# A masked-autoencoder loss on one core: squares over pairs of columns, loads and engine orders from a timetable

## The chip, the core and the metric

The kernel runs on one core of a Trainium2 chip. The metric is the time of one execution on the device, in microseconds (us), as the median of several runs. Engines are named as the profile names them: PE multiplies matrices, PEld loads its weights, DVE is VectorE, ACT is ScalarE, POOL is GpSimd, SP is SyncE. Loads from HBM run on 16 DMA engines; POOL or SP issues them.

## What is computed

Two fp32 arrays of 32 x 147 rows with 768 values each come in, `pred` and `target`. Each target row is normalised by its own mean and variance, the squared difference to the prediction row is averaged, and then the 147 rows of a batch entry are averaged:

```python
mean = target.mean(axis=-1, keepdims=True)
var = target.var(axis=-1, keepdims=True)
target = (target - mean) / np.sqrt(var + 1e-6)
loss = np.mean((pred - target) ** 2, axis=-1)
return loss.mean(axis=-1).astype(np.float32)
```

## The kernel before

**Tiling.** Four rows of each batch entry lie side by side, so 32 x 4 = 128 partitions hold one row each. This text calls one such set of 128 rows, 768 values wide, a *column*. There are 36 full columns (0 to 35) and a rest, column 36, of 32 x 3 = 96 rows. The target is loaded in pieces: the rest, then nine pieces of four columns, named t0, t4 up to t32 in the program by their first column. The prediction comes as the rest (p36), eight pieces of four columns (p0 to p28), one of two (p32) and two of one (p34, p35). The profile cuts the numbers off and writes `t` and `p`. `load` (L60) issues every piece from POOL, and the DMA turns fp32 into bf16 on the way.

**One column's way.** `stats` (L113) takes a group, as a rule four columns: for each of them DVE makes two half-row statistics (L125) and joins them (L126); ACT takes the square root of the group's variances (L127, out `r`); DVE makes the reciprocal (L129) and minus mean times reciprocal (L130, `nmr`). `normalise` (L140) then has POOL write the normalised column `s` in bf16 (L147). `losses` (L156) has PE subtract: two passes over the column, of 512 and 256 values each, one with minus the identity on `s` and one with the identity on `p`, into a PSUM tile `z` of two banks (L167; three such tiles). ACT squares `z` and sums it along the row into one value of `rl` (L169); reading the accumulator is a second record in the profile. After each prediction piece PE sums `rl` over the rows of a batch entry by a mask, into `acc` (L173). At the end DVE adds the four columns of `acc` (L190) and SP stores 32 values (L191).

**Order.** Every engine executes its instructions in order. The calls are written piece by piece: statistics and normalisation of one target piece, then subtraction, squares and the sum of the prediction piece that is due. `pin` (L57) fixes the place of the loads and normalisations on POOL; the rest is placed by the framework's scheduler. The loads stand in the order t36, t0, p36, t4, t8, p0, t12, p4 and so on; eight are issued at the start, and further ones at the first and fourth normalisation of a group (L150). There are eight semaphores for POOL's loads: each issue from the ninth on waits until the load eight before it has landed, if that is not known yet.

Of the kernel before, what the change touches and what calls it, by code (L numbers as in the profile page):

```python
# [14 lines left out]
def kernel(  # L15
# [7 lines left out]
    nc = tc.nc  # L23
    B, N, D = pred.shape
# [8 lines left out]
    BANK = 512  # L33

# [3 lines left out]
    def main_rows(x, k0, k1):  # L38
        return bass.AP(tensor=x.tensor, offset=x.offset + k0 * D,
                       ap=[[N * D, B], [KJ * D, J], [1, (k1 - k0) * D]])  # L40

    def rest_rows(x):
        return bass.AP(tensor=x.tensor, offset=x.offset + KM * D,
                       ap=[[N * D, B], [KJ * D, J - 1], [1, D]])

    data = ctx.enter_context(tc.tile_pool(name="data", bufs=1))
    work = ctx.enter_context(tc.tile_pool(name="work", bufs=20))
    small = ctx.enter_context(tc.tile_pool(name="small", bufs=6))
    singles = ctx.enter_context(tc.tile_pool(name="singles", bufs=1))
    psum = ctx.enter_context(tc.tile_pool(name="psum", bufs=3, space=bass.MemoryType.PSUM))  # L50
# [6 lines left out]
    pin = tc.keep_in_program_order  # L57
    tbuf, pbuf = {}, {}

    def load(kind, piece):  # L60
        x = targ_f if kind == "t" else pred_f
        k0, k1 = piece if piece else (KM, KM + 1)
        rows = P if piece else RP
        dt = BF16 if kind == "t" else BF16
        til = data.tile([P, (k1 - k0) * D], dt, name=f"{kind}{k0}")
        eng = nc.gpsimd if kind == "t" else nc.gpsimd
        pin(eng.dma_start(out=til[:rows], in_=main_rows(x, k0, k1) if piece else rest_rows(x)))  # L67
        for k in range(k0, k1):
            (tbuf if kind == "t" else pbuf)[k] = (til, (k - k0) * D, rows)

    eps_t = singles.tile([P, 1], F32)
    nc.vector.memset(eps_t, eps)  # L72

    load("t", t_pieces[0])
    load("t", t_pieces[1])
    load("p", p_pieces[0])
    load("t", t_pieces[2])
    load("t", t_pieces[3])
# [3 lines left out]
    for til, v in ((ident, 1.0), (nident, -1.0)):  # L82
        nc.gpsimd.memset(til, 0.0)
        nc.gpsimd.affine_select(out=til, in_=til, compare_op=ALU.not_equal, fill=v,  # L84
                                base=0, pattern=[[-1, P]], channel_multiplier=1)
    masks = {}
    for name, per, rows in (("main", J, P), ("rest", J - 1, RP)):
        m = singles.tile([P, B], F32, name=f"mask_{name}")
        nc.gpsimd.memset(m, 1.0 / (N * D))
        nc.gpsimd.affine_select(out=m[:rows], in_=m[:rows], compare_op=ALU.is_ge, fill=0.0,  # L90
                                base=0, pattern=[[-per, B]], channel_multiplier=1)
        nc.gpsimd.affine_select(out=m[:rows], in_=m[:rows], compare_op=ALU.is_ge, fill=0.0,
                                base=per - 1, pattern=[[per, B]], channel_multiplier=-1)
        masks[name] = m

    seq = []
    for i in range(4, len(t_pieces)):
        seq += [("p", p_pieces[i - 3]), ("t", t_pieces[i])]
    seq += [("p", q) for q in p_pieces[len(t_pieces) - 3:]]
    todo = iter(seq)  # L100

    def load_next():
        nxt = next(todo, None)
        if nxt is not None:
            load(*nxt)

    for _ in range(3):
        load_next()

    acc = psum1.tile([B, 4], F32)  # L110
    rs = {}

    def stats(piece):  # L113
        k0, k1 = piece if piece else (KM, KM + 1)
        rows = P if piece else RP
        K = k1 - k0
        r = small.tile([P, K], F32, name="r")
        nmr = small.tile([P, K], F32, name="nmr")
        if norm_pix_loss:
            mv = small.tile([P, K, 2], F32, name="mv")  # L120
            for k in range(k0, k1):
                til, o, _ = tbuf[k]
                st = small.tile([P, 2, 6], F32, name="st")
                for j in range(2):
                    nc.vector.bn_stats(out=st[:rows, j, :], in_=til[:rows, o + j * half:o + (j + 1) * half])  # L125
                nc.vector.bn_aggr(out=mv[:rows, k - k0], in_=st[:rows])  # L126
            nc.scalar.activation(out=r[:rows], in_=mv[:rows, :, 1], func=ACTF.Sqrt,  # L127
                                 bias=eps_t[:rows], scale=1.0)
            nc.vector.reciprocal(out=r[:rows], in_=r[:rows])  # L129
            nc.vector.scalar_tensor_tensor(out=nmr[:rows], in0=mv[:rows, :, 0], scalar=-1.0,  # L130
                                           in1=r[:rows], op0=ALU.mult, op1=ALU.mult)
        else:
            nc.vector.memset(r, 1.0)
            nc.vector.memset(nmr, 0.0)
        for k in range(k0, k1):
            rs[k] = (r[:rows, k - k0:k - k0 + 1], nmr[:rows, k - k0:k - k0 + 1])

    sbuf = {}

    def normalise(piece):  # L140
        k0, k1 = piece if piece else (KM, KM + 1)
        rows = P if piece else RP
        for k in range(k0, k1):
            r, nmr = rs[k]
            til, o, _ = tbuf[k]
            s = work.tile([P, D], BF16, name="s")
            pin(nc.gpsimd.tensor_scalar(out=s[:rows], in0=til[:rows, o:o + D], scalar1=r, scalar2=nmr,  # L147
                                        op0=ALU.mult, op1=ALU.add))
            sbuf[k] = s
            if k == k0 or k == k0 + 3:  # L150
                load_next()

    n_acc = [0]
    total_acc = len(p_pieces)

    def losses(piece):  # L156
        k0, k1 = piece if piece else (KM, KM + 1)
        rows = P if piece else RP
        K = k1 - k0
        rl = small.tile([P, 4], F32, name="rl")  # L160
        for k in range(k0, k1):
            s = sbuf[k]
            ptil, po, _ = pbuf[k]
            z = psum.tile([P, 2 * BANK], F32, name="z")
            for src, so, w, first in ((s, 0, nident, True), (ptil, po, ident, False)):
                for c0, c1 in ((0, BANK), (BANK, D)):
                    nc.tensor.matmul(z[:rows, c0:c1], w[:rows, :rows], src[:rows, so + c0:so + c1],  # L167
                                     start=first, stop=not first)
            nc.scalar.activation(out=z[:rows, :D], in_=z[:rows, :D], func=ACTF.Square,  # L169
                                 accum_out=rl[:rows, k - k0:k - k0 + 1])  # L170
        if K < 4:
            nc.vector.memset(rl[:, K:], 0.0)
# [13 lines left out]
    for pp in p_pieces[len(t_pieces) - 1:]:  # L186
        losses(pp)
# [39 lines left out]
```

## Time and profile before

| | us |
|---|---|
| median of 3 runs | 89.34 (89.18 to 89.64) |
| the profiled execution | 89.54 |
| its span, first to last instruction | 87.8 |
| busy: PE / DVE / ACT / POOL | 41.1 / 43.4 / 35.3 / 49.7 |

Numbers of the trace are microseconds from the span's start. A timeline row reads: start, length, engine, line, operation, out<-in, count, and in brackets the idle time of the engine before it with what ended it. A row of the waits reads: who waited, for whom, then total, number of times, longest. A chain row reads: start, length, what. A row of a table by stretch reads: the stretch, its length, busy time and number of records, granted PE clock, share of the DMA engines, GB/s written. A group row reads: line, engine, operation, out<-in, shapes, count, then busy us, mean ns of one, and idle time before.

### The profile page before, as it was taken

The numbers are of one execution on the slowest core, as the hardware profiler recorded it, in microseconds if no ns is written. First come the engines' busy times: TensorE is split into PE (matmuls) and PEld (weight loads), VectorE is DVE, ScalarE is ACT, GpSimd is POOL, SyncE is SP. The second block draws the span as 40 slices with busy tenths as digits, with TensorE's granted clock in tenths as the row PEclk, the third lists the DMA queues.
The fourth block names the chain that finished last, engine by engine and source line by source line (L and its number), as shares of the span: only waits on it lengthen the run. The fifth ranks groups of instructions, "written<-read, shape, count | busy, mean of one in ns | idle before, by whom it ended". The sixth has DMA issues, their size and how long they took to land.

```text
span 87.8 us, 755 instructions
## 1 busy us (share of the span) xinstructions
PE 41.1 (47%) x172; PEld 18.4 (21%) x172; DVE 43.4 (49%) x139; ACT 35.3 (40%) x86; POOL 49.7 (57%) x73
## 2 busy tenths in 40 slices
PE   0000060000495349659847255962005998999400
PEld 0000020000241124214214012420003544454200
DVE  0051989999598379339609817930991000000000
ACT  5010001010501940780492095050084678999900
POOL 4994332999999998398089469339428600000000
PEclk9999999999999955555589965579555569999995
DMA  0899999999999999999999999999999940000000
GB/s 0 120 213 201 216 216 213 218 213 216 216 208 224 213 216 213 210 224 213 216 210 214 221 218 213 207 217 222 216 213 202 202 72 0 0 0 0 0 0 0
DMA packets 3156, 14.49 MB, mean 165 GB/s; under 512 B 400, under 2 KB 848, under 8 KB 3152
## 3 DMA queue, kind: packets, MB, share of 16 engines
q0 software_dynamic: 3104, 14.45, 81.2%
q14 instruction: 3, 0.02, 0.1%
q8 instruction: 1, 0.02, 0.1%
q1 hardware_dynamic: 48, 0.00, 0.0%
HBM read 28.90 MB, written 0.00 MB: 329 GB/s over the span
## 4 chain that ended last, share of the span: by engine, by line
DMA 42%; POOL 18%; DVE 11%; ACT 9%; PE 7%; issue 6%; ACTq 1%; POOLq 0%
DMA t<-in_target_dram 42%; POOL s L147 13%; ACT z L169 9%; DVE st L125 9%; PE z L167 7%; POOL t L67 3%; POOL p L67 2%; DVE mv L126 1%; PE acc L173 1%; ACTq L222 1%; DVE nmr L130 1%; DVE r L129 0%; DVE ob L190 0%; ACTq L169 0%; ACT r L127 0%
## 5 line engine op out<-in xcount | busy, mean ns | idle before, releaser
L147 POOL TENSOR_SCALAR s<-t,r,nmr 128x768 bf16<-128x768 bf16 (+1 forms) x37 | 35.9, 977 | 18.6 <-DVE nmr L130 17.8
L125 DVE BATCH_NORM_STATS2 st<-t 128x6 f32<-128x384 bf16 (+1 forms) x74 | 36.5, 529 | 19.1 <-DMA t<-in_target_dram 19.1
L167 PE MATMUL z<-s,nident 128*128 128x512 bf16 (+1 forms) x74 | 24.9, 429 | 17.9 <-POOL s L147 11.2
L169 ACT ACTIVATE z<-z 128x768 f32<-128x768 f32 (+1 forms) x37 | 29.3, 792 | 3.0 <-PE z L167 2.9
L167 PE MATMUL z<-p,ident 128*128 128x512 bf16 (+1 forms) x74 | 24.8, 426 | 0.0
L127 ACT ACTIVATE r<-mv,eps_t 128x4 f32<-128x4 f32 (+2 forms) x11 | 3.2, 295 | 44.2 <-DVE mv L126 44.2
L167 PEld LDWEIGHTS <-nident 128*128 128x128 bf16 (+1 forms) x74 | 7.3, 117 | 26.9 <-ACT z L169 10.9
L167 PEld LDWEIGHTS <-ident 128*128 128x128 bf16 (+1 forms) x74 | 9.4, 126 | 8.7 <-issue 5.4
L173 PE MATMUL acc<-rl,mask_main 128*32 128x4 f32 x22 | 2.6, 190 | 13.9 <-ACT z L169 13.8
L190 DVE TENSOR_REDUCE ob<-acc 32x1 f32<-32x4 f32 x1 | 0.1, 150 | 16.2 <-PE acc L173 16.2
L126 DVE BATCH_NORM_AGGREGATE mv<-st 128x2 f32<-128x12 f32 (+1 forms) x37 | 7.2, 195 | 0.3
L67 POOL DMA_DIRECT2D p<-in_pred_dram x12 | 6.9, 572 | 0.0
L169 ACT ACTIVATION_READ_ACCUMULATOR z<-z 128x1 f32 (+1 forms) x37 | 6.9, 185 | 0.0
L67 POOL DMA_DIRECT2D t<-in_target_dram x10 | 5.8, 595 | 0.8 <-POOLq L208 0.8
L173 PEld LDWEIGHTS acc<-rl,mask_main 128*32 128x32 f32 x22 | 1.7, 119 | 18.1 <-ACT z L169 18.1
L173 PE MATMUL acc<-rl,mask_rest 96*32 96x4 f32 x2 | 0.3, 205 | 10.6 <-ACT z L169 10.6
L129 DVE RECIPROCAL r<-r 128x4 f32<-128x4 f32 (+2 forms) x11 | 1.9, 172 | 3.5 <-ACT r L127 3.5
L130 DVE SCALAR_TENSOR_TENSOR nmr<-mv,r 128x4 f32<-128x4 f32 (+2 forms) x11 | 3.1, 282 | 0.2
L173 PEld LDWEIGHTS acc<-rl,mask_rest 96*32 96x32 f32 x2 | 0.2, 140 | 11.3 <-ACT z L169 11.3
L127 ACT ACT_TABLE_LOAD x1 | 1.3, 1283 | 0.8 <-PEq L208 0.8
L72 DVE MEMSET eps_t<- 128x1 f32 x1 | 0.1, 59 | 0.9 <-PEq L208 0.9
L84 POOL TENSOR_SCALAR_AFFINE_SELECT ident<-ident 128x128 bf16<-128x128 bf16 x1 | 0.4, 389 | 0.0
(14 smaller groups left out, 2.9 us busy)
## 6 DMA issues: line engine op xcount, KB each, us to landing
t<-in_target_dram POOLq DMA_DIRECT2D x9, 768.0 KB, 19.4
p<-in_pred_dram POOLq DMA_DIRECT2D x8, 768.0 KB, 22.6
p<-in_pred_dram POOLq DMA_DIRECT2D x1, 384.0 KB, 25.3
p<-in_pred_dram POOLq DMA_DIRECT2D x2, 192.0 KB, 21.4
t<-in_target_dram POOLq DMA_DIRECT2D x1, 144.0 KB, 3.1
p<-in_pred_dram POOLq DMA_DIRECT2D x1, 144.0 KB, 6.8
out_dram<-ob SPq DMA_DIRECT2D x1, 0.1 KB, 3.2
```

Source lines behind the costliest of these rows:

```text
L67: pin(eng.dma_start(out=til[:rows], in_=main_rows(x, k0, k1) if piece else rest_rows(x)))
L84: nc.gpsimd.affine_select(out=til, in_=til, compare_op=ALU.not_equal, fill=v, base=0, pattern=[[-1, P]], channel_multiplier=1)
L125: nc.vector.bn_stats(out=st[:rows, j, :], in_=til[:rows, o + j * half:o + (j + 1) * half])
L126: nc.vector.bn_aggr(out=mv[:rows, k - k0], in_=st[:rows])
L127: nc.scalar.activation(out=r[:rows], in_=mv[:rows, :, 1], func=ACTF.Sqrt, bias=eps_t[:rows], scale=1.0)
L129: nc.vector.reciprocal(out=r[:rows], in_=r[:rows])
L130: nc.vector.scalar_tensor_tensor(out=nmr[:rows], in0=mv[:rows, :, 0], scalar=-1.0, in1=r[:rows], op0=ALU.mult, op1=ALU.mult)
L147: pin(nc.gpsimd.tensor_scalar(out=s[:rows], in0=til[:rows, o:o + D], scalar1=r, scalar2=nmr, op0=ALU.mult, op1=ALU.add))
L167: nc.tensor.matmul(z[:rows, c0:c1], w[:rows, :rows], src[:rows, so + c0:so + c1], start=first, stop=not first)
L169: nc.scalar.activation(out=z[:rows, :D], in_=z[:rows, :D], func=ACTF.Square, accum_out=rl[:rows, k - k0:k - k0 + 1])
L173: nc.tensor.matmul(acc, masks["main" if piece else "rest"][:rows], rl[:rows], start=n_acc[0] == 0, stop=n_acc[0] == total_acc - 1)
L222: with _tile.TileContext(nc) as tc:
```

## The change

The program is written as single steps (a load, a group's statistics, a column's normalisation, a unit's subtraction, a unit's square, a sum). A small calculation with assumed durations gives each step a planned time; the steps are then written out sorted by it, and every instruction is pinned, so that each engine's order is the timetable's. Beside that:

- PE and ACT work on *units*: pairs of neighbouring columns, and single columns for the rest and the last two. A pair's `z` is 1536 values over three PSUM banks, in two buffers instead of three of two banks. PE writes it in six matmuls of 512 instead of eight of 512 and 256; ACT squares it in one instruction.
- `s` tiles are as wide as a pair, ten instead of twenty.
- The first two target pieces (t36 and t0) are issued by SyncE ("hw") and stay fp32. All others stay on POOL ("sw").
- The last target piece is split in two (t32 and t34), p28 into p28 and p30, and p24 is loaded ahead of t34. Groups of statistics hold four columns up to column 27, two from there on.
- All row sums of full columns go to one tile `rl`. The first 15 units are summed by one matmul, the rest column by one, the last four units by one each: 6 sums instead of 12. The zero fills of `rl` are gone. `acc` has 15 columns instead of 4.
- Constants are made after the first eight loads of POOL.

```diff
-    t_pieces = [None] + [(k, k + 4) for k in range(0, KM, 4)]
-    p_pieces = [None] + [(k, k + 4) for k in range(0, KM - 4, 4)] + [(KM - 4, KM - 2), (KM - 2, KM - 1), (KM - 1, KM)]
+    stream = [("t", REST, REST + 1, "hw"), ("t", 0, 4, "hw"), ("p", REST, REST + 1, "sw")]
+    stream += [("t", 4, 8, "sw"), ("t", 8, 12, "sw"), ("p", 0, 4, "sw")]
+    for c in range(12, KM - 4, 4):
+        stream += [("t", c, c + 4, "sw"), ("p", c - 8, c - 4, "sw")]
+    stream += [("t", KM - 4, KM - 2, "sw"), ("p", KM - 12, KM - 8, "sw"), ("t", KM - 2, KM, "sw"),
+               ("p", KM - 8, KM - 6, "sw"), ("p", KM - 6, KM - 4, "sw"), ("p", KM - 4, KM - 2, "sw"),
+               ("p", KM - 2, KM - 1, "sw"), ("p", KM - 1, KM, "sw")]
+
+    units = [(REST,)] + [(c, c + 1) for c in range(0, KM - 2, 2)] + [(KM - 2,), (KM - 1,)]
+
+    groups = [(REST,)] + [tuple(range(c, c + 4)) for c in range(0, KM - 8, 4)]
+    groups += [(c, c + 1) for c in range(KM - 8, KM, 2)]
...
+        til = data.tile([P, (c1 - c0) * D], F32 if q == "hw" else BF16, name=f"{kind}{c0}")
+        eng = nc.sync if q == "hw" else nc.gpsimd
+        pin(eng.dma_start(out=til[:n], in_=dram(x, c0, c1)))
...
+            at(lanes[k % 8] + (0.01 * k), lambda piece=piece: load(*piece))
+            lanes[k % 8] = issue[i] + 0.2
...
+    def subtract(u):
+        n, W = rows_of(u[0]), len(u) * D
+        z = psum.tile([P, 3 * BANK], F32, name="z")
...
+        for src, so, w, first in ((s, 0, nident, True), (ptil, po, ident, False)):
+            for a in range(0, W, BANK):
+                b = min(a + BANK, W)
+                pin(nc.tensor.matmul(z[:n, a:b], w[:n, :n], src[:n, so + a:so + b], start=first, stop=not first))
+
+    def square(u):
...
+        pin(nc.scalar.activation(out=z[:n, :W], in_=z[:n, :W], func=ACTF.Square, accum_out=to))
+
+    def sums(a, b):
+        if a == "rest":
+            pin(nc.tensor.matmul(acc[:, 0:1], mask_rest[:RP], rl_rest[:RP], start=False, stop=False))
         else:
...
+            pin(nc.tensor.matmul(acc[:, 0:b - a], mask, rl[:, a:b], start=a == 0, stop=b == len(main_units)))
...
+    for g in groups:
+        dve = max([dve] + [land["t", c] for c in g])
+        at(dve, lambda g=g: stats(g))
+        dve += 1.26 * len(g) + 0.8
...
+        pe = max([pe, free[0]] + [ready[c] for c in u] + [land["p", c] for c in u])
+        at(pe, lambda u=u: subtract(u))
...
+    for when, order, fn in sorted(todo, key=lambda e: e[:2]):
+        fn()
```

**Where instructions stand, first place: ACT towards the end.** `r` rows are square roots of a group (128x4 four columns, 128x2 two), `z` rows squares. Before, from the root of columns 20 to 23 on:

```order
L127 ACTIVATE r<-mv,eps_t 128x4 [waits DVE_49,Pool_49]
L169 ACTIVATE z,rl<-z 128x768 [waits PE_49,Activation_49] x4
L127 ACTIVATE r<-mv,eps_t 128x4 [waits DVE_49,Pool_49]
L169 ACTIVATE z,rl<-z 128x768 [waits PE_49,Activation_49]
L127 ACTIVATE r<-mv,eps_t 128x2 [waits DVE_49,Pool_49]
L169 ACTIVATE z,rl<-z 128x768 [waits PE_49,Activation_49] x3
L127 ACTIVATE r<-mv,eps_t 128x2 [waits DVE_49,Pool_49]
L169 ACTIVATE z,rl<-z 128x768 [waits PE_49,Activation_49] x16
```

After, from the roots of columns 28, 29 and 30, 31 on:

```order
L142 ACTIVATE r<-mv,eps_t 128x2 [waits DVE_49,Pool_49] x2
L184 ACTIVATE z,rl<-z 128x1536 [waits PE_49,Activation_49]
L142 ACTIVATE r<-mv,eps_t 128x2 [waits DVE_49,Pool_49]
L184 ACTIVATE z,rl<-z 128x1536 [waits PE_49,Activation_49] x2
L142 ACTIVATE r<-mv,eps_t 128x2 [waits DVE_49,Pool_49]
L184 ACTIVATE z,rl<-z 128x1536 [waits PE_49,Activation_49] x4
L184 ACTIVATE z,rl<-z 128x768 [waits PE_49,Activation_49] x2
```

Behind the last root, of columns 34 and 35, stood 16 squares of one column; now four squares of two columns stand there, (26, 27) to (32, 33), and two of one. The root of (34, 35) stands directly behind the square of (24, 25).

**Second place: POOL at the start.** The names carry their first column and a running number. Before:

```order
L67 DMA t36_75<-in_target_dram 96x1x768
L67 DMA t0_77<-in_target_dram 128x1x3072
L67 DMA p36_79<-in_pred_dram 96x1x768
L67 DMA t4_81<-in_target_dram 128x1x3072
L67 DMA t8_83<-in_target_dram 128x1x3072
L83 MEMSET ident_85 128x128
L83 MEMSET nident_86 128x128
```

After:

```order
L89 DMA p36_85<-in_pred_dram 96x1x768
L89 DMA t4_87<-in_target_dram 128x1x3072
L89 DMA t8_89<-in_target_dram 128x1x3072
L89 DMA p0_91<-in_pred_dram 128x1x3072
L89 DMA t12_93<-in_target_dram 128x1x3072
L89 DMA p4_95<-in_pred_dram 128x1x3072
L89 DMA t16_97<-in_target_dram 128x1x3072
L89 DMA p8_99<-in_pred_dram 128x1x3072
L112 MEMSET ident_73 128x128
```

t36 and t0 have left POOL for SP, and eight loads instead of five stand ahead of the constants.

**Third place: the sums on PE.** Before, a sum stands among the matmuls of the fourth piece from the end; p_379 is the piece p28:

```order
L167 MATMUL z<-s,nident 128x256
L167 LDWEIGHTS ident
L167 MATMUL z<-p_379,ident 128x512
L173 MATMUL acc<-rl,mask_main 32x4 [waits Activation_49]
L167 LDWEIGHTS ident
L167 MATMUL z<-p_379,ident 128x256
```

After, all sums stand behind the prediction pass of column 34 (p_445); that of column 35 (p_473) is the last piece:

```order
L178 MATMUL z<-p_445,ident 128x256
L190 MATMUL acc<-rl,mask 32x15
L188 MATMUL acc<-rl_rest,mask_rest 32x1
L178 LDWEIGHTS nident [waits Activation_49]
L178 MATMUL z<-s,nident 128x512 [waits Pool_49]
...
L178 MATMUL z<-p_473,ident 128x256
L190 MATMUL acc<-rl,mask 32x1 x2
L190 MATMUL acc<-rl,mask 32x1 [waits Activation_49] x2
```

A sum that waits for ACT in mid-stream is gone; the ones left stand at the end, two of them waiting.

More of the change, by code (lines that the diff above doesn't have):

```diff
@@ L96 @@
[L96 to L116, printed above, removed]
+    mask = singles.tile([P, B], F32)
@@ L117, in stats @@
+    at(1.0, constants)
+    def stats(g):
+        n, K = rows_of(g[0]), len(g)
         r = small.tile([P, K], F32, name="r")
         nmr = small.tile([P, K], F32, name="nmr")
[L119 to L131, printed above, removed]
-        else:
-            nc.vector.memset(r, 1.0)
-            nc.vector.memset(nmr, 0.0)
@@ L153 @@
[L153 to L172, printed above, removed]
-        nc.tensor.matmul(acc, masks["main" if piece else "rest"][:rows], rl[:rows],
-                         start=n_acc[0] == 0, stop=n_acc[0] == total_acc - 1)
-        n_acc[0] += 1
```

174 lines of the change are left out of this document (108 added, 66 removed).

## The prediction

> **What bounds the kernel now.** I read the page first (busy shares and slices), then the chain in order of time, then the waits, then timelines of single engines. No engine is full over the span; the DMA engines are, but only to about 71 us of 87.8:
>
> ```profile
> span 87.8 us, 755 instructions
> PE 41.1 (47%) x172; PEld 18.4 (21%) x172; DVE 43.4 (49%) x139; ACT 35.3 (40%) x86; POOL 49.7 (57%) x73
> DMA  0899999999999999999999999999999940000000
> ```
>
> So there are two stages: a stream of loads, and a tail of some 16 us in which nothing is loaded. The profiled execution took 89.54 us, 1.74 more than its span, and lies 0.2 above the median of 89.34. The tail belongs to ACT, as the busy time of the squares alone shows from 64.1 us on (L169; x counts two records each, the square and the reading of its accumulator):
>
> ```profile
> 64.10:83.50 19.40, 16.02 (x38) 0.80 0.38 74
> ```
>
> 38 records are 19 of 37 squares: by 64.1 us only 18 are done. Why they are late stands in the waits (total, times, longest) and in the chain:
>
> ```profile
> ACT r L127 <- DVE mv L126: 44.2, 10, 7.6
> PE acc L173 <- ACT z L169: 24.4, 9, 10.6
> ```
>
> ```profile
> 34.32 26.94 DMA t<-in_target_dram
> ...
> 61.28 1.48 DVE st L125 x3
> ...
> 63.95 0.04 ACT r L127
> ...
> 82.41 0.82 ACT z L169 x2
> ```
>
> ACT runs in order and spends 44.2 us at a square root whose statistics are not there yet, with squares behind it whose data are. PE stands 24.4 us at a small sum (acc) that waits for ACT, with subtractions behind it. The last target piece is seen at 61.28, the root at 63.95, and from there the squares run nearly without a gap to the end. They, not the loads, set the end.
>
> **The change part by part.** The columns are worth a time each on the DMA. Two starts of DVE on target pieces, three pieces apart:
>
> ```profile
> 31.36 1.48 DVE L125 BATCH_NORM_STATS2 st<-t 128x6 f32<-128x384 bf16 x3 [2.01 <-DMA t<-in_target_dram]
> ...
> 53.29 1.02 DVE L125 BATCH_NORM_STATS2 st<-t 128x6 f32<-128x384 bf16 x2 [2.25 <-DMA t<-in_target_dram]
> ```
>
> (53.29 - 31.36)/3 = 7.31 us for four target and four prediction columns, 0.914 a column. The bytes read stay the same, so the stream keeps its length. It can begin earlier, because SyncE now issues the first two pieces:
>
> ```profile
> SPq L208 <- PEq L208: 0.7, 1, 0.7
> ```
>
> ```profile
> 1.36 1.25 POOL L67 DMA_DIRECT2D t<-in_target_dram  x2 [0.85 <-POOLq L208]
> ```
>
> SyncE is free at 0.7, POOL's first issue was at 1.36: the gain is 0 to 0.66; I take 0.3. The last target piece (columns 34, 35) now has four prediction columns (24 to 27) before it that stood behind it: 61.28 + 4 x 0.914 - 0.3 = 64.64. The later prediction pieces follow at 66.47 (28, 29), 68.30, 70.12, 71.04 (34) and 71.95 (35).
>
> *DVE.* The pinned order puts each aggregation right behind its own two statistics. The first column of before runs that way; the others show what follows the last aggregation:
>
> ```profile
> 4.47 1.02 DVE L125 BATCH_NORM_STATS2 st<-t 96x6 f32<-96x384 bf16 x2 [3.51 <-DMA t<-in_target_dram]
> ...
> 5.52 0.20 DVE L126 BATCH_NORM_AGGREGATE mv<-st 96x2 f32<-96x12 f32 x1
> ```
>
> ```profile
> 33.75 0.19 DVE L126 BATCH_NORM_AGGREGATE mv<-st 128x2 f32<-128x12 f32 x1
> 33.85 0.97 DVE L125 BATCH_NORM_STATS2 st<-t 128x6 f32<-128x384 bf16 x2
> ...
> 35.39 0.21 DVE L126 BATCH_NORM_AGGREGATE mv<-st 128x2 f32<-128x12 f32 x1
> 35.63 0.30 ACT L127 ACTIVATE r<-mv,eps_t 128x4 f32<-128x4 f32 x1 [3.81 <-DVE mv L126]
> 35.96 0.18 DVE L129 RECIPROCAL r<-r 128x4 f32<-128x4 f32 x1 [0.36 <-ACT r L127]
> 36.17 0.16 DVE L130 SCALAR_TENSOR_TENSOR nmr<-mv,r 128x4 f32<-128x4 f32 x1
> ```
>
> A column is 5.52 - 4.47 + 0.10 = 1.15; a root starts 0.24 after its last aggregation starts; root to end of nmr is 36.17 + 0.16 - 35.63 = 0.70. A group of four costs 4 x 1.15 - 0.10 + 0.24 + 0.70 = 5.44, a pair 3.14. So the root of (34, 35) starts at 64.64 + 1.15 + 1.05 + 0.24 = 67.08. Statistics read from fp32 have no row; I take the bf16 price (double would be the other end, four columns, early, where DVE has slack to be counted below).
>
> *ACT.* In its order this last root stands ahead of the square of (26, 27) and all later ones, so they start at 67.28 (0.20 later, as below). Two squares of 768 columns take two periods; the rows give one period (82.32 - 81.50 = 0.82):
>
> ```profile
> 63.95 0.29 ACT L127 ACTIVATE r<-mv,eps_t 128x2 f32<-128x2 f32 x1 [5.04 <-DVE mv L126]
> 64.15 0.79 ACT L169 ACTIVATE z<-z 128x768 f32<-128x768 f32 x1
> ...
> 81.50 0.79 ACT L169 ACTIVATE z<-z 128x768 f32<-128x768 f32 x1
> ...
> 82.32 0.79 ACT L169 ACTIVATE z<-z 128x768 f32<-128x768 f32 x1
> ```
>
> A square of 1536 columns has no row. It costs at most two periods, 1.63; at least one period plus 768 columns at the slope between the 2-wide root (0.29) and the square (0.79), 0.50, so 1.31. Both ends are equally far; I take the middle, 1.47.
>
> *PE.* One pass of 768 columns has two prices, by the granted clock: 0.64 from start to start in one stretch, 0.33 in another.
>
> ```profile
> 46.59 0.23 PE L173 MATMUL acc<-rl,mask_main 128*32 128x4 f32 x2 [1.51 <-ACT z L169]
> ...
> 47.08 0.49 PE L167 MATMUL z<-p,ident 128*128 128x512 bf16 x2
> 47.41 0.49 PE L167 MATMUL z<-s,nident 128*128 128x512 bf16 x2
> ...
> 51.50 0.82 PE L167 MATMUL z<-s,nident 128*128 128x512 bf16 x2 [2.63 <-ACT z L169]
> ...
> 67.56 0.85 PE L167 MATMUL z<-p,ident 128*128 128x512 bf16 x2
> 68.20 0.85 PE L167 MATMUL z<-s,nident 128*128 128x512 bf16 x2
> 68.50 0.80 ACT L169 ACTIVATE z<-z 128x768 f32<-128x768 f32 x1 [1.62 <-PE z L167]
> ```
>
> The pass begun at 67.56 releases ACT at 68.50: 0.64 and 0.30 of handover. With two pair-sized buffers instead of three single ones, PE can begin a unit only when the square two units back is done; then it needs four passes and the handover, 1.62 at the fast clock.
>
> *The sum.* Squares start: (26, 27) 67.28; (28, 29) 68.75; (30, 31) when its buffer, free at 68.75, is filled: 70.37; (32, 33) 71.84; 34 at 73.31; 35 when the buffer free at 73.31 is filled by two passes, 73.31 + 0.66 + 0.30 = 74.27. From the last square's start to the span's end before: 87.8 - 82.32 = 5.48, of work that the change leaves as it is (last sum, reduction, output). Span 79.75, time 79.75 + 1.74 = 81.5. With 1.31 or 1.63 for a pair it is 0.5 less or more.
>
> *POOL and the queues.* Eight loads are now issued in a row ahead of the constants (before: five, and three behind them), later ones at planned places among the normalisations:
>
> ```profile
> L147 POOL TENSOR_SCALAR s<-t,r,nmr 128x768 bf16<-128x768 bf16 x36 | 34.9, 977 | 16.0 <-DVE nmr L130 15.2 <-DVE rl L172 0.3
> ...
> L67 POOL DMA_DIRECT2D p<-in_pred_dram x12 | 6.9, 572 | 0.0
> ```
>
> Normalisations keep their number, 22 loads at 0.57 stay on POOL. Four normalisations and one to two issues per 7.31 us are 4 x 0.98 + 2 x 0.57 = 5.1: hidden behind the stream. Each later issue waits for the load eight before it, and a normalisation behind it waits along; that load is old by then, seven loads are still queued (some 25 us), so neither runs dry. Constants come about 2 us later than before and the first matmul needs them only after the first normalisation: nothing. POOL reading fp32 has no row either; five normalisations even at twice 0.98 would be 5 us in the first 25, where PE waits for prediction columns 0 to 3 anyway. The removed zero fills of rl (4 on DVE) and 6 of 12 sums on PE are worth what PE no longer waits for at them, which is in the sum.
>
> *A rule against the trace, first:* all loads of before run on one queue.
>
> ```profile
> q0 software_dynamic: 3104, 14.45, 81.2%
> ...
> q1 hardware_dynamic: 48, 0.00, 0.0%
> ```
>
> Nothing shows what two queues with work do to each other. Target columns 0 to 3 were seen at 8.48 in before; now at 8.2 if SyncE's pieces go first, or, if the queues share evenly, up to 4.75 columns later, 12.5. The Trainium skill ("DMA: Bandwidth & Descriptors", Queues, rings and completion order) says that each DMA engine takes turns between the queues that have work, packet by packet; by that it is the 12.5. The sum is the same with both: from 12.5, seven groups of 5.44 end at 50.6, and columns 28 to 31 land at 53.0 (53.29 - 0.3). The delay is worked off with 2.4 us to spare.
>
> ```profile
> 8.48 1.02 DVE L125 BATCH_NORM_STATS2 st<-t 128x6 f32<-128x384 bf16 x2 [2.75 <-DMA t<-in_target_dram]
> ```
>
> **The rivals.**
>
> *A, the slow PE clock in the tail.* For it: PE will stand idle from about 67.1 (second half of (28, 29)) to 68.75, 1.6 us. The trace kept the fast clock over a gap of 1.51 (46.59) and had the slow one after 2.63 (51.50). With passes of 0.64, a fill is 2.86: (30, 31) 71.61, (32, 33) 74.17, 34 at 75.64, 35 at 77.22: 77.22 + 5.48 + 1.74 = 84.4. Against it: columns 20 to 23 land at 56.6 by the same count, and from there PE finds work. The Trainium skill ("TensorE: Matmul & The Clock Gate", Part 1) puts the loss of clock at an idle window of about 3.4 us; the gap of 2.63 speaks against that as a limit, but by it the tail stays fast and the time 81.5.
>
> *B, DVE becomes the bound.* If sharing delays the first columns to 12.5 and a column costs 1.35 instead of 1.15 (fp32, or POOL's issues in its way), a group is 6.24: columns 28 to 31 begin at 56.2, three pairs at 3.54 bring the last to 66.8 instead of 64.64, and its own two columns take 0.4 longer, all +2.6: 84.1. Against it: only five columns are fp32.
>
> *C, the queue on ACT dissolves.* If the root of (34, 35) comes early enough or pairs are cheap, only the last column counts: 71.95 + 0.33 + 0.30 + 5.48 + 1.74 = 79.8, and 79.4 with the full 0.66 at the start.
>
> *D, slower than before: roots behind squares.* ACT now holds two squares ahead of each root, and DVE waits at the reciprocal for the root. The two squares and a root take 2 x 1.47 + 0.20 = 3.14 of a group's 5.44, so 2.3 us are free. From the point where both squares come more than 2.3 us late in each group, every group grows by the rest; to pass 90 us it takes 8.5 + 2.4 us over seven groups, squares 3.9 late in each. Eight slow passes instead of fast ones are 2.5 late: at the edge, not beyond. And the prediction piece of those squares stands ahead of the target piece of that root in the stream.
>
> **How the numbers follow.** A measurement of this kernel tells about 0.5% (0.45 us) from no change. Forecast 0.62 (79.9 to 83.2), A 0.16, C 0.10, B 0.07, D 0.03, and 0.02 that the gains are lost in some other way and the time stays. The range runs from C's lower end, 79.4, to A with the dear pair, 84.4 + 0.5 = 84.9. Faster: 0.62 + 0.16 + 0.10 + 0.07 = 0.95; same 0.02; slower 0.03.
>
> **What would show it.** Right: the last loads end near 71.5, the last root near 67, six squares in a row behind it, a pair near 1.47, and the output's issue near 75.7 (83.72 before). Wrong: passes of 0.64 behind the last root (A), DVE without idle time at columns 28 to 31 (B), roots that wait for squares in mid-stream (D), or a stream that ends later than before's.
>
> ```profile
> 83.72 0.38 SPq L191 DMA_DIRECT2D out_dram<-ob  x1
> ```

## The result, and the profile after

| | before | after |
|---|---|---|
| median, us | 89.42 (89.18 to 89.64) | 81.1 (80.73 to 81.13) |
| the profiled execution, us | 89.54 | 80.73 |
| its span | 87.8 | 79.0 |

The ratio is 0.906, with a 95% interval of 0.901 to 0.910. The forecast was 81.5. Executions over 1.5% above the fastest of the same kernel (82.38 here) are in no median, range or difference below, though the 4.7 us that one expectation names counts them, and the profiled ones of three experiments (the sums in mid-stream, the root one place later, ACT unpinned) are such, so their rows are read for order and waits, not for the time.

The page of after, with the span, the DMA engines in 40 slices and the two queues:

```profile
span 79.0 us, 602 instructions
DMA  0799999999999999999999999999999999990000
...
q0 software_dynamic: 3136, 13.52, 84.2%
q1 hardware_dynamic: 304, 1.87, 6.2%
```

A slice is 1.98 us here and was 2.20 before. The stream again ends at 71 us or so, but only four empty slices follow it, 8 us, where seven stood before, some 15. The same in windows around its end (length, then busy times, granted clock, DMA share, GB/s), after:

```profile
70.00:71.00 1.00, 1.00 (x6) 0.34 (x4) 0.00 (x0) 1.00 (x1) 0.00 (x0) 1.00 0.82 150
71.00:72.00 1.00, 0.76 (x5) 0.31 (x4) 0.00 (x0) 1.00 (x3) 0.00 (x0) 1.00 0.05 9
```

and before:

```profile
70.00:71.00 1.00, 1.00 (x5) 0.51 (x4) 0.00 (x0) 0.69 (x2) 0.00 (x0) 0.50 1.04 184
71.00:72.00 1.00, 1.00 (x5) 0.50 (x4) 0.00 (x0) 0.90 (x2) 0.00 (x0) 0.65 0.14 23
```

The loads end some 0.3 us earlier; the gain is not there. It is in the work behind them. The waits of after:

```profile
ACT r L142 <- DVE mv L141: 39.4, 12, 9.8
...
ACT z L184 <- PE z L178: 2.0, 5, 1.0
...
PE acc L190 <- ACT z L184: 0.8, 1, 0.8
```

PE's 24.4 us at the small sum are 0.8 now. ACT still waits 39.4 us at its roots: it is idle for more than half of the stream either way, and that total says little by itself. What counts is what stands behind the last root, in ACT's timeline of after:

```profile
66.45 0.29 ACT L142 ACTIVATE r<-mv,eps_t 128x2 f32<-128x2 f32 x1 [1.66 <-DVE mv L141]
66.66 1.43 ACT L184 ACTIVATE z<-z 128x1536 f32<-128x1536 f32 x1
...
68.11 1.43 ACT L184 ACTIVATE z<-z 128x1536 f32<-128x1536 f32 x1
...
69.83 1.44 ACT L184 ACTIVATE z<-z 128x1536 f32<-128x1536 f32 x1 [0.17 <-PE z L178]
...
71.28 1.44 ACT L184 ACTIVATE z<-z 128x1536 f32<-128x1536 f32 x1
...
72.72 0.80 ACT L184 ACTIVATE z<-z 128x768 f32<-128x768 f32 x1
...
73.80 0.80 ACT L184 ACTIVATE z<-z 128x768 f32<-128x768 f32 x1 [0.16 <-PE z L178]
```

Six squares stand there. The last root of before, also of columns 34 and 35, was not the one at 63.95 that the prediction shows (columns 32 and 33, on which ACT waited), but the next:

```profile
66.60 0.28 ACT L127 ACTIVATE r<-mv,eps_t 128x2 f32<-128x2 f32 x1
```

(The list of ACT's order ahead of the prediction begins, for before, at the root of columns 24 to 27, not 20 to 23.) From this last root to the start of the last square were 82.32 - 66.60 = 15.72 us before, with 16 squares, and are 73.80 - 66.45 = 7.35 now. The 8.37 less there, 0.15 by which the root is earlier, and 0.28 less behind the last square (79.0 - 73.80 = 5.20 for 5.48) are the 8.8 us between the spans.

### The profile page after: what moved, and what is told of

Same layout as the page of the kernel before. It is cut to its first block, busy times and chain, and to the rows that moved or that the text cites. A ratio compares the mean times of both kernels' runs of the same rounds, so it can differ in the third digit from the quotient of the medians.

```text
span 79.0 us, 602 instructions
## 1 busy us (share of the span) xinstructions
PE 38.7 (49%) x126; PEld 13.4 (17%) x126; DVE 45.7 (58%) x137; ACT 32.5 (41%) x53; POOL 50.1 (63%) x73
## 4 chain that ended last, share of the span: by engine, by line
DMA 42%; DVE 31%; ACT 7%; POOL 5%; PE 4%; issue 4%; SPq 1%; ACTq 0%
DMA p<-in_pred_dram 30%; DVE st L140 23%; DMA t<-in_target_dram 12%; DVE mv L141 5%; ACT z L184 5%; POOL s L158 5%; PE z L178 4%; ACT r L142 2%; DVE r L143 1%; DVE nmr L144 1%; SPq L89 1%; POOL t L89 1%; PE acc L190 0%; DVE ob L224 0%; ACTq L256 0%
## 5 line engine op out<-in xcount | busy, mean ns | idle before, releaser
L140 DVE BATCH_NORM_STATS2 st<-t 128x6 f32<-128x384 bf16 (+2 forms) x74 | 36.3, 533 | 14.4 <-DMA t<-in_target_dram 14.4
L158 POOL TENSOR_SCALAR s<-t,r,nmr 128x768 bf16<-128x768 bf16 (+2 forms) x37 | 35.9, 976 | 13.3 <-DVE nmr L144 13.0
L178 PE MATMUL z<-s,nident 128*128 128x512 bf16 (+3 forms) x57 | 21.4, 492 | 26.6 <-POOL s L158 23.7
L184 ACT ACTIVATE z<-z 128x1536 f32<-128x1536 f32 (+2 forms) x20 | 26.7, 1336 | 2.0 <-PE z L178 2.0
L178 PE MATMUL z<-p,ident 128*128 128x512 bf16 (+3 forms) x57 | 20.6, 478 | 8.9 <-DMA p<-in_pred_dram 8.9
L142 ACT ACTIVATE r<-mv,eps_t 128x4 f32<-128x4 f32 (+2 forms) x12 | 3.6, 296 | 39.4 <-DVE mv L141 39.4
L178 PEld LDWEIGHTS <-nident 128*128 128x128 bf16 (+1 forms) x57 | 5.8, 117 | 39.5 <-ACT z L184 16.3
L178 PEld LDWEIGHTS <-ident 128*128 128x128 bf16 (+1 forms) x57 | 7.0, 123 | 20.5 <-issue 17.8
L184 ACT ACTIVATION_READ_ACCUMULATOR z<-z 128x1 f32 (+1 forms) x20 | 3.7, 186 | 0.0
L144 DVE SCALAR_TENSOR_TENSOR nmr<-mv,r 128x4 f32<-128x4 f32 (+2 forms) x12 | 1.9, 161 | 0.4
L190 PE MATMUL acc<-rl,mask 128*32 128x1 f32 (+1 forms) x10 | 0.8, 179 | 0.8 <-ACT z L184 0.8
```

Source lines behind the costliest of these rows:

```text
L140: pin(nc.vector.bn_stats(out=st[:n, j, :], in_=til[:n, o + j * half:o + (j + 1) * half]))
L142: pin(nc.scalar.activation(out=r[:n], in_=mv[:n, :, 1], func=ACTF.Sqrt, bias=eps_t[:n], scale=1.0))
L144: pin(nc.vector.scalar_tensor_tensor(out=nmr[:n], in0=mv[:n, :, 0], scalar=-1.0, in1=r[:n], op0=ALU.mult, op1=ALU.mult))
L158: pin(nc.gpsimd.tensor_scalar(out=s[:n, so:so + D], in0=til[:n, o:o + D], scalar1=r, scalar2=nmr, op0=ALU.mult, op1=ALU.add))
L178: pin(nc.tensor.matmul(z[:n, a:b], w[:n, :n], src[:n, so + a:so + b], start=first, stop=not first))
L184: pin(nc.scalar.activation(out=z[:n, :W], in_=z[:n, :W], func=ACTF.Square, accum_out=to))
```

## The experiments

The theory after the result was that of the forecast: the end is the last root on ACT and the queue of squares behind it, so the engine orders carry the gain. The rivals: the sums that left PE's stream carry it; or DVE's order; or the wide squares. The changed kernel is run again, and eleven runs undo one part at a time, do one alone, or go a step beyond. "The end" is the start of the last square.

**The changed kernel again**, beside the first three of the others.

> The changed kernel as it is, as the measure for the others on the same chip. Every theory: 80.7 to 81.4 us, last square begun near 73.8 us of the span.

Measured 81.03 (80.74 to 81.46), span 79.4, root at 66.53, end at 73.87. Differences below are from these. The kernel before, run beside each of these, had medians of 89.4 to 89.6, so 0.3 us or less is not read as a difference.

**Squares of single columns.**

```diff
-    psum = ctx.enter_context(tc.tile_pool(name="psum", bufs=2, space=bass.MemoryType.PSUM))
+    psum = ctx.enter_context(tc.tile_pool(name="psum", bufs=3, space=bass.MemoryType.PSUM))
...
-    units = [(REST,)] + [(c, c + 1) for c in range(0, KM - 2, 2)] + [(KM - 2,), (KM - 1,)]
+    units = [(REST,)] + [(c,) for c in range(KM)]
...
-        z = psum.tile([P, 3 * BANK], F32, name="z")
+        z = psum.tile([P, 2 * BANK], F32, name="z")
```

> Undoes one part: all units are single columns, squares of 768, three PSUM buffers of two banks; timetable, loads and sums stay. Theory (the end is set by the last square root at 66.45 us and by the squares that stand behind it on ACT): eleven squares instead of four wide and two narrow ones stand behind that root; 66.66 + 10 x 0.82 = 74.9 for the last start against 73.8, so about 1.0 us more than the changed kernel, 82.1. Rival (the saving is ACT's work as a whole: 17 pairs at 0.17 us less each): 2.9 us more, 84.0. Rival (pairs cost as much as they save, because two wide buffers make PE wait): no difference.

Measured 83.59 (82.89 to 83.7), +2.6. DVE's start on the last target piece:

```profile
64.89 1.02 DVE L140 BATCH_NORM_STATS2 st<-t 128x6 f32<-128x384 bf16 x2 [2.50 <-DMA t<-in_target_dram]
```

and ACT from there on, the root and the first and last of the squares behind it:

```profile
67.37 0.30 ACT L142 ACTIVATE r<-mv,eps_t 128x2 f32<-128x2 f32 x1 [2.52 <-DVE mv L141]
67.57 0.79 ACT L184 ACTIVATE z<-z 128x768 f32<-128x768 f32 x1
...
75.73 0.79 ACT L184 ACTIVATE z<-z 128x768 f32<-128x768 f32 x1
```

Root to end takes 8.36 us, 1.0 more than 7.35: what was expected of the queue. The target piece was seen at 64.89, 0.85 later than in the changed kernel (64.04), and the root with it. Why the piece comes later was not found; the piece of columns 28 to 31 was still seen at 53.04, as in the changed kernel (53.01). The two parts make up 1.9 of the 2.0 us that the profiled span (81.4) is longer; the medians differ by 0.6 more.

**All loads on POOL.**

```diff
-    stream = [("t", REST, REST + 1, "hw"), ("t", 0, 4, "hw"), ("p", REST, REST + 1, "sw")]
+    stream = [("t", REST, REST + 1, "sw"), ("t", 0, 4, "sw"), ("p", REST, REST + 1, "sw")]
```

> Undoes one part: the first two target pieces go through POOL's queue as bf16 again. Theory (the end moves with the stream of loads, and SyncE starts it earlier): the stream begins up to 0.55 us later (first issue at 1.36 instead of 0.81 us), and all landings and the end with it, 0.3 to 0.6 us more, about 81.5. Rival (sharing between the two queues delays target columns 0 to 3 and with it DVE, so the fp32 pieces cost): the same or up to 0.5 us less, DVE's first four columns near 8.5 instead of 11.3 us.

Measured 81.31 (81.26 to 81.7), +0.3 with overlapping intervals (ratios 0.910 and 0.907, each within 0.004). In the profile the root stands at 66.85, 0.32 later. Both fit the 0.3 at which the head start was priced, but the difference is not clear of noise.

**Coarse pieces at the end**: t32 and p28 whole again, p24 behind the last target piece, and the group (28 to 31) of four.

```diff
-    for c in range(12, KM - 4, 4):
+    for c in range(12, KM, 4):
...
-    stream += [("t", KM - 4, KM - 2, "sw"), ("p", KM - 12, KM - 8, "sw"), ("t", KM - 2, KM, "sw"),
-               ("p", KM - 8, KM - 6, "sw"), ("p", KM - 6, KM - 4, "sw"), ("p", KM - 4, KM - 2, "sw"),
+    stream += [("p", KM - 8, KM - 4, "sw"), ("p", KM - 4, KM - 2, "sw"),
...
```

> Undoes one part: the last loads as before the change (one target piece of four columns at 32, prediction columns 24 to 27 behind it, 28 to 31 as one piece). Theory: the last root hardly moves (four columns land near 60.7 us, two groups of statistics bring the root to 66.3), but columns 24 and 25 are squared only after 64.6 + 1.0 and 28 to 31 land at 68.2; the last square starts 0.3 to 0.8 us later, time 81.4 to 81.9. Rival (the finer pieces are what shortens the tail): 2 us or more, above 83.

Measured 82.18 (81.99 to 82.76), +1.1, more than the 0.9 at most that was expected. ACT, the last root and the last square:

```profile
65.76 0.29 ACT L141 ACTIVATE r<-mv,eps_t 128x2 f32<-128x2 f32 x1 [2.79 <-DVE mv L140]
...
74.81 0.80 ACT L183 ACTIVATE z<-z 128x768 f32<-128x768 f32 x1 [0.16 <-PE z L177]
```

The root is 0.77 earlier, but five pairs stand behind it instead of four: root to end 9.05.

**Order left to the scheduler** on ACT, DVE and PE (`pin` taken off their instructions; POOL's order, pairs, pieces and sums stay).

```diff
-                pin(nc.vector.bn_stats(out=st[:n, j, :], in_=til[:n, o + j * half:o + (j + 1) * half]))
+                free_(nc.vector.bn_stats(out=st[:n, j, :], in_=til[:n, o + j * half:o + (j + 1) * half]))
...
-        pin(nc.scalar.activation(out=z[:n, :W], in_=z[:n, :W], func=ACTF.Square, accum_out=to))
+        free_(nc.scalar.activation(out=z[:n, :W], in_=z[:n, :W], func=ACTF.Square, accum_out=to))
```

> Undoes one part: only loads and normalisations are pinned, as before the change; DVE, ACT and PE get the framework's order again. Pairs, pieces, SyncE loads and late sums stay. Theory (the order on ACT is the gain): behind the last root, at 66.5 us, stand seven pairs and two singles instead of four and two; last start 66.7 + 7 x 1.46 + 0.82 = 77.7 instead of 73.8 us, about 4 us more, 85. Rival (wide squares, finer pieces and late sums carry the gain, the order is free): 81 to 82.

Measured 86.74 (86.26 to 87.23), +5.7 where 4 was expected. ACT:

```profile
66.77 0.28 ACT L143 ACTIVATE r<-mv,eps_t 128x2 f32<-128x2 f32 x1
66.96 1.44 ACT L185 ACTIVATE z<-z 128x1536 f32<-128x1536 f32 x1
...
79.28 0.80 ACT L185 ACTIVATE z<-z 128x768 f32<-128x768 f32 x1 [0.16 <-PE z L179]
```

The root is where it was; seven pairs and two singles stand behind it, 12.5 us. The orders carry about two thirds of the gain of 8.4. Which engine's?

**Only ACT unpinned.**

```diff
-        pin(nc.scalar.activation(out=r[:n], in_=mv[:n, :, 1], func=ACTF.Sqrt, bias=eps_t[:n], scale=1.0))
+        free_(nc.scalar.activation(out=r[:n], in_=mv[:n, :, 1], func=ACTF.Sqrt, bias=eps_t[:n], scale=1.0))
...
-        pin(nc.scalar.activation(out=z[:n, :W], in_=z[:n, :W], func=ACTF.Square, accum_out=to))
+        free_(nc.scalar.activation(out=z[:n, :W], in_=z[:n, :W], func=ACTF.Square, accum_out=to))
```

> The changed kernel with DVE, PE and POOL in the timetable's order and only ACT's order left to the framework's scheduler. Behind the last root then stand seven squares of pairs and two of single columns instead of four and two; the roots of columns 4 to 15 stand ahead of all main squares. Theory (ACT's order by itself bears on the end: the squares behind the last root are the end): root near 66.5 as in the changed kernel, then 7 x 1.45 + 2 x 0.80 instead of 4 x 1.45 + 2 x 0.80 with the waits for buffers gone where ACT is full, so 3 x 1.45 less about 0.3 later: 85 us (84.3 to 85.6). Rival (with DVE in the timetable's order the normalised columns are early, PE and ACT find their work, and ACT's order is worth little): below 82.5 us, with squares done early and gaps on ACT at the end. If PE is held at the slow clock by the longer waits for buffers, above 86.

Measured 86.38 (85.97 to 87.03), +5.3; the rival (below 82.5) is out, and the theory's 85.6 at most was too little. ACT:

```profile
67.81 0.29 ACT L143 ACTIVATE r<-mv,eps_t 128x2 f32<-128x2 f32 x1
68.02 1.43 ACT L185 ACTIVATE z<-z 128x1536 f32<-128x1536 f32 x1
...
80.34 0.80 ACT L185 ACTIVATE z<-z 128x768 f32<-128x768 f32 x1 [0.16 <-PE z L179]
```

Root to end 12.53, 5.2 more than 7.35, from ACT's order alone. The PE clock is not it: it was granted in full from 62.1 to the end of the squares. What the order does shows in PE's waits:

```profile
PE z L179 <- ACT z L185: 23.1, 11, 11.9
```

In the scheduler's order the roots of columns 0 to 19 stand ahead of the first square of a pair, which starts at 38.84; in the changed kernel those of columns 0 to 11 do, and it starts at 26.87. So the two buffers of z stay full up to 11.9 us long, and PE, which could subtract, stands at a buffer. In the changed kernel the longest such wait was 1.6.

**Only ACT pinned**, DVE and PE left to the scheduler.

> Like the kernel whose DVE, ACT and PE are ordered by the framework (86.7), but ACT keeps the timetable's order; DVE and PE remain free. Theory (ACT's order is the one that costs): back to 81 to 82. Rival (the order of PE or DVE costs as much): 84 or more.

Measured 86.25 (86.05 to 86.56), +5.2: the theory that ACT's order suffices fell. PE's order differs from the changed kernel's only behind the last pair, where the sums stand one column earlier and wait for nothing, so this is put down to DVE's; no run frees DVE alone. Its order in the changed kernel behind the statistics of columns 24 to 27 (t24, group 383) runs on with their own reciprocal and `nmr`:

```order
L141 BN_AGGR mv_385<-st_398 128x2
L143 RECIPROCAL r_383<-r_383 128x4
L144 SCALAR_TENSOR_TENSOR nmr_384<-mv_385,r_383 128x4
L140 BN_STATS st_434<-t28_236 128x6 x2
```

With DVE unpinned the same two stand behind the statistics of columns 32 and 33 (t32), six columns later; `nmr` starts at 60.90 instead of 50.94:

```order
L141 BN_STATS st_491<-t32_284 128x6
L142 BN_AGGR mv_486<-st_491 128x2
L144 RECIPROCAL r_383<-r_383 128x4
L145 SCALAR_TENSOR_TENSOR nmr_384<-mv_385,r_383 128x4
L141 BN_STATS st_522<-t34_356 128x6 x2
```

The longest such delay is early. The root of columns 4 to 7 was done by 20.6, their reciprocal stood behind later statistics until 35.23, and POOL waited for it, where its longest wait for DVE in the changed kernel is 3.4:

```profile
POOL s L159 <- DVE r L144: 14.0, 1, 14.0
```

So POOL gets the factors late, PE gets `s` late, and ACT stands at squares with the last root behind them. ACT's timeline:

```profile
66.02 1.44 ACT L185 ACTIVATE z<-z 128x1536 f32<-128x1536 f32 x1 [1.36 <-PE z L179]
...
69.13 0.29 ACT L143 ACTIVATE r<-mv,eps_t 128x2 f32<-128x2 f32 x1
70.23 1.44 ACT L185 ACTIVATE z<-z 128x1536 f32<-128x1536 f32 x1 [0.81 <-PE z L179]
...
79.12 0.80 ACT L185 ACTIVATE z<-z 128x768 f32<-128x768 f32 x1 [0.16 <-PE z L179]
```

The statistics of the last target piece began at 64.01, as in the changed kernel; its root came 2.6 us later than there.

**Sums in mid-stream**, two units at a time as soon as their square is planned done; the rest as in the changed kernel.

```diff
-    acc = psum1.tile([B, early], F32)
+    acc = psum1.tile([B, 2], F32)
...
-        if i == early - 1:
-            at(act + 3.0, lambda: sums(0, early))
-            at(act + 3.0, lambda: sums("rest", None))
+        if i == 1:
+            at(asq, lambda: sums(0, 2))
+            at(asq, lambda: sums("rest", None))
+        elif 1 < i < early and i % 2 == 1:
+            at(asq, lambda i=i: sums(i - 1, i + 1))
...
```

> Undoes one part: the first 14 units' sums stand on PE in mid-stream again, one behind every second pair, each waiting for that pair's square; the last sums stay at the end; acc has two columns. Theory (before, the small sums on PE only passed ACT's lateness on): PE waits at each of the seven sums, but has idle time there; the end moves by less than 0.4 us, 80.7 to 81.5. Rival (PE held at the sums is what made the kernel before late): 3 us or more, above 84.

Measured 85.07 (two executions, 84.52 and 85.61), +4.0; the theory (81.5 at most) fell and its rival was right. The waits, and PE near the end:

```profile
PE acc L190 <- ACT z L184: 19.5, 8, 6.2
...
ACT z L184 <- PE z L178: 9.7, 11, 3.1
```

```profile
64.05 0.27 PE L190 MATMUL acc<-rl,mask 128*32 128x2 f32 x2 [3.80 <-ACT z L184]
64.25 1.46 PE L178 MATMUL z<-s,nident 128*128 128x512 bf16 x3
```

The sum waits for a square which stands behind a root, and the subtractions behind the sum wait too; then ACT waits for PE. Two engines that run in order take turns. PE's fills are slow on top (1.46 for three matmuls, 0.82 in the changed kernel).

**The same sums one pair later**, so that a sum asks for a square done long before.

```diff
+        if 2 <= i < early and i % 2 == 0:
+            at(max(pe, act) + 0.001, lambda i=i: sums(i - 2, i))
...
```

> Like the kernel with sums in mid-stream, but each of the seven sums stands one pair later on PE, so that PE has written the next pair when it waits for the square. Theory now (a sum right behind its pair makes PE and ACT take turns, since PE can write nothing ahead; with long idle times PE also falls to its slow clock): most of the 4.7 us goes, 81 to 82.5. Rival (any sum in mid-stream that waits for ACT costs, as in the kernel before): 84 or more.

Measured 81.60 (two executions, 81.54 and 81.66), +0.6; the ratio to before is 0.913 (0.908 to 0.919). Most of the 4.0 is gone though the sums stand in mid-stream, and PE's waits at them fell from 19.5 us to 2.3. It was the wait at them, not the sums.

**The kernel before with its sums at the end**, each with a tile of its own for what it sums; nothing else changed.

```diff
-        nc.tensor.matmul(acc, masks["main" if piece else "rest"][:rows], rl[:rows],
-                         start=n_acc[0] == 0, stop=n_acc[0] == total_acc - 1)
-        n_acc[0] += 1
+        late.append((masks["main" if piece else "rest"][:rows], rl[:rows]))
...
+    for i, (m, v) in enumerate(late):
+        pin(nc.tensor.matmul(acc, m, v, start=i == 0, stop=i == total_acc - 1))
```

> One part alone: the kernel before the change, with its 12 sums moved behind all subtractions, nothing else. Theory: ACT's order is unchanged, 16 squares stand behind the last root, so the time stays within 1 us of before, 88.4 to 89.5. Rival (the sums on PE): most of the gain, 81 to 84.

Measured 86.86 (86.36 to 87.22), 2.8 less than before beside it (89.64), between both expectations. ACT's order is before's, with 16 squares behind the last root:

```profile
66.04 0.28 ACT L128 ACTIVATE r<-mv,eps_t 128x2 f32<-128x2 f32 x1
...
79.94 0.79 ACT L170 ACTIVATE z<-z 128x768 f32<-128x768 f32 x1
```

Root to end is 13.90, 1.8 less than before's 15.72; the last root is 0.56 earlier, and so was the last target piece. The sums alone give about a third of the gain; the queue on ACT stays.

**Target pieces earlier**: the last eight target columns in four pieces, with the prediction pieces moved behind them.

```diff
+    stream += [("t", c, c + 2, "sw") for c in (KM - 8, KM - 6)] + [("p", KM - 16, KM - 14, "sw")]
+    stream += [("t", c, c + 2, "sw") for c in (KM - 4, KM - 2)]
+    stream += [("p", c, c + 2, "sw") for c in range(KM - 14, KM - 2, 2)] + [
...
```

> One step beyond the changed kernel: the last target columns 28 to 35 are loaded in pairs ahead of prediction columns 22 to 35, and those in pairs, so that the last root is done some 4 us earlier and only the arrival of prediction pieces is left. Theory (root, then the queue on ACT): the last root near 62, squares follow their pieces every 1.83 us without a queue; 33's piece lands near 69.4, the last square starts at about 72.7 instead of 73.8, 80.0 us. Rival (the end is set by the last loads alone, landed at 71.2): no difference from the changed kernel, or, if two more issues on POOL and smaller pieces slow the stream, 0.5 us more.

Measured 83.22 (82.63 to 83.43), +2.2 where -1 was expected. DVE needs its time for the pieces: the last four roots follow each other by 3.1 to 3.5 us, about the 3.14 at which a pair was priced, so the last comes at 64.32, 2.2 earlier but not near 62, and six pairs and two singles stand behind it. And PE, short of prediction pieces, lost its clock:

```profile
61.20 0.81 PE L179 MATMUL z<-p,ident 128*128 128x512 bf16 x3 [2.83 <-DMA p<-in_pred_dram]
...
63.07 1.44 PE L179 MATMUL z<-p,ident 128*128 128x512 bf16 x3 [0.15 <-DMA p<-in_pred_dram]
66.13 1.46 PE L179 MATMUL z<-s,nident 128*128 128x512 bf16 x3 [1.62 <-ACT z L185]
```

**The last root one square later** on ACT: a single instruction moves.

```diff
-        dve = max([dve] + [land["t", c] for c in g])
+        dve = max([dve] + [land["t", c] for c in g]) + (2.0 if g == groups[-1] else 0.0)
```

> The changed kernel with one instruction moved: on ACT the square root of columns 34, 35 stands behind the square of (26, 27) instead of ahead of it; no other engine's order changes. Theory (the root at 66.45 us and the queue behind it set the end): that square is ready at 65.0 and fits into ACT's idle 1.7 us before the root; one wide square fewer stands behind the root, but 28 to 33 then wait for their pieces; last start 72.9 instead of 73.8, 0.9 us less, 80.1 us. Rival (the loads, or the two wide buffers, set the end): within 0.2 us of the changed kernel, 81.0.

Measured 80.95 (80.56 to 81.37), the changed kernel's time; the rival was right. In its profile, of an execution of 82.11 us whose target pieces came 1.7 us later or more (the last at 65.78), PE's waits are for the last prediction pieces:

```profile
67.65 0.81 PE L178 MATMUL z<-p,ident 128*128 128x512 bf16 x3 [0.18 <-DMA p<-in_pred_dram]
...
69.51 0.81 PE L178 MATMUL z<-p,ident 128*128 128x512 bf16 x3 [0.33 <-DMA p<-in_pred_dram]
...
73.18 0.48 PE L178 MATMUL z<-p,ident 128*128 128x512 bf16 x2 [0.67 <-DMA p<-in_pred_dram]
```

There the root has ceased to bound, and the loads do. That they take back all of the gain in an execution at the median too is argued, not shown: there is no trace of one. No run was clearly faster than the changed kernel.

## Why the prediction was right, point by point

**Which queue sets the end: right.** The last root and six squares in a row, as forecast. ACT's order alone moves the time by 5.3, through the number of squares behind that root (12.5 us with seven pairs and two singles).

**The sum: right, with small errors that partly cancel.** The forecast had the root at 67.08, the last square 7.19 later, 5.48 from there to the span's end. Measured: 66.45, 7.35 and 5.20. -0.63 + 0.16 - 0.28 = -0.75, and 79.75 - 0.75 = 79.0.

**The landing of the last target piece: 0.67 too late.** DVE in after:

```profile
52.94 1.02 DVE L140 BATCH_NORM_STATS2 st<-t 128x6 f32<-128x384 bf16 x2 [1.93 <-DMA t<-in_target_dram]
...
63.97 1.02 DVE L140 BATCH_NORM_STATS2 st<-t 128x6 f32<-128x384 bf16 x2 [1.70 <-DMA t<-in_target_dram]
```

The head start was right: 53.29 - 52.94 = 0.35 for 0.3. The base was wrong: the step set out from one row, 61.28, which stood 7.99 us behind 53.29 where eight columns take 7.31. The same piece was seen at 60.72 in the kernel before with its sums at the end. Counted from 52.94 instead, twelve columns at 0.914 give 63.91.

**Pair square and PE's fill: right.** 68.11 - 66.66 = 1.45 for 1.47. The gap that rival A needed came, and the fast clock stayed (why, is in the last section: the forecast weighed the length of the gap, which does not decide):

```profile
68.26 0.82 PE L178 MATMUL z<-s,nident 128*128 128x512 bf16 x3 [1.60 <-ACT z L184]
68.92 0.81 PE L178 MATMUL z<-p,ident 128*128 128x512 bf16 x3
```

A pass of 1536 values takes 0.66 there.

**DVE: priced right.** A column takes 1.12 to 1.18, from fp32 as from bf16, and POOL's column 0.97 to 0.98 from either. Rival B is out. The second row is target columns 0 to 3, the third columns 20 to 23:

```profile
4.51 1.02 DVE L140 BATCH_NORM_STATS2 st<-t 96x6 f32<-96x384 f32 x2 [3.58 <-DMA t<-in_target_dram]
...
11.26 1.02 DVE L140 BATCH_NORM_STATS2 st<-t 128x6 f32<-128x384 f32 x2 [4.78 <-DMA t<-in_target_dram]
...
38.29 1.02 DVE L140 BATCH_NORM_STATS2 st<-t 128x6 f32<-128x384 bf16 x2 [0.49 <-DMA t<-in_target_dram]
```

The two queues do share: 11.26, between 8.2 and 12.5 and nearer to the latter, where all loads on POOL give 8.37. The Trainium skill's rule ("DMA: Bandwidth & Descriptors", Queues, rings and completion order), that each engine takes turns between queues with work, agrees. By 38.29 DVE waits for a load again: the delay is worked off, as forecast, and costs nothing at the end.

**POOL hidden: right in the end.** One issue on POOL did wait 3.2 us for a load, early, and nothing at the end shows it:

```profile
POOL p L89 <- DMA t<-in_target_dram: 3.2, 1, 3.2
```

**What the forecast did not say.** It priced DVE's new order by its length per group and left its place out: the old order puts a group's `nmr` behind statistics of later columns, and undoing it costs 5.2. It put the removed sums into "what PE no longer waits for at them, which is in the sum" without a price: back in mid-stream at their squares they cost 4.0. So part of the agreement is luck: the sum has no term for where these instructions stand, and with DVE's left in the scheduler's order (86.25) it would have come out nearly 5 us short. The costs of 5.3, 5.2 and 4.0 exceed the gain of 8.4 and cannot be added; the orders of ACT, DVE and PE undone together cost 5.7, hardly more than one of them. That fits engines that hand two buffers, factors and sums around, so that the worst order sets the end, and it fits the 2.8 of the sums alone. Rival C (79.8, the queue dissolves) stays unreached by the two tries, at 80.95 and 83.22.

**Open.** Why single columns bring the last target piece 0.85 later, so that of the 2.6 that pairs are worth only the 1.0 of the queue is explained; and what an execution at the median of the kernel with the later root waits for.

## What to carry to other kernels

Where engines run in order, find the last wait that every late unit stands behind, and count the units behind it: that count times the price of one is the tail. A good order on one engine is worth little while a neighbour's puts a result behind later work, so pin all engines that hand buffers around, and place a small reduction well behind what it reads. Base the landing of a piece on the spacing of several, not on one row. To keep PE's clock, count its work per stretch of 3.4 us (last section), not the length of a gap.

## What the runs showed of the hardware

**PE's granted clock changed only on a grid of 3.4 us.** Read in tenths of a microsecond, the changes in after fall at 40.0, 46.9, 50.3, 53.7, 57.1 and 60.5; in all fourteen traces, from the first change in the trace to the end of the work, each comes 3.4 us or a multiple of it after the one before. The change went with how long PE had been busy in the stretch between two such instants:

| kernel, stretch, us | PE busy in it, us | clock in it | clock behind it |
|---|---|---|---|
| after, 46.9 to 50.3 | 1.24 | full | half |
| after, 50.3 to 53.7 | 3.32 | half | full |
| after, 53.7 to 57.1 | 0.48 | full | half |
| after, 60.5 to 63.9 | 2.05 | full | full |
| after, 67.4 to 70.8 | 2.54 | full | full |
| before, 44.4 to 47.8 | 1.89 | full | full |
| before, 47.8 to 51.2 | 1.07 | full | half |
| before, 51.2 to 54.6 | 2.05 | half | half |
| sums in mid-stream, 45.4 to 48.8 | 0.98 | full | half |

Full is 1.00 in the windows of the profile, half 0.50. Ahead of its first change a trace shows the full clock even where passes are slow (after, 1.44 us for three matmuls at 19.91). From the first change on, the full clock was lost in those traces behind every stretch with 1.44 us of work or less and kept behind every one with 1.63 or more; it came back behind every one with 2.72 or more and behind none with 2.42 or less. The length of a gap alone does not decide: in the kernel with sums in mid-stream the passes behind a gap of 1.85 (47.32, 0.82 for three matmuls) were fast and those behind the next, of 1.81 (49.96, 1.44), slow. The gap of 1.60 in the tail of after fits: PE worked for 2.54 us of its stretch. The Trainium skill ("TensorE: Matmul & The Clock Gate", Part 1) names a free-running window of about 3.4 us, and the grid agrees; it lets the clock fall after an idle window, where here up to 1.44 us of work did not keep it.
